# Stores begun by ScalarE's queue instead of SyncE's in a conformer, state-space and FFN block

## The chip, the cores and the metric

The kernel runs on one core of one Trainium2 chip. The metric is the device time of one execution in microseconds (us); the median of several runs is compared. Lower is better.

## The reference

One block of a streaming encoder works on 1024 tokens of width 1024, in float32. Its first half normalises the input, projects it, and runs two branches side by side: a gated convolution over 31 tokens with a layer norm, and a Mamba-2 scan (SSD) with 32 heads in 4 groups. Gates merge them. Its second half is a SwiGLU FFN. Both halves are modulated by the vector c (adaLN). Cut to what matters:

```python
shift, scale, gate = adaln(c, w_ada_mix, b_ada_mix)
h = rms_norm(x, norm_mix_w) * (1.0 + scale) + shift
conv_in, z, xbc, dt_raw, g_conv, g_ssm = split(h @ w_in)
u = a_half * sigmoid(b_half)                       # halves of conv_in
u = silu(layer_norm(causal_depthwise_conv(u, conv_dw_w, conv_dw_b)))
y_conv = u @ w_conv_out
xs, bm, cm = split(silu(causal_depthwise_conv(xbc, ssm_conv_w, ssm_conv_b)))
y = ssd_chunked_scan(xs, softplus(dt_raw + dt_bias), -exp(a_log), bm, cm) + d_skip * xs
y = group_rms_norm(y * silu(z)) * ssm_norm_w
y_ssm = y @ w_ssm_out
x = x + gate * ((sigmoid(g_conv) * y_conv + sigmoid(g_ssm) * y_ssm) @ w_out)
...
x = x + gate * ((silu(h @ w_gate) * (h @ w_up)) @ w_ffn_down)
return rms_norm(x, final_norm_w)
```

## The kernel before, in words

Channels lie on the 128 partitions and tokens in the free dimension. The tokens come in two halves of 512 (`hf` 0 and 1), so nearly every tile is 128x512. Each float32 product is made of three matmuls of rounded parts (`mm3`, L175 to L189): weight high by data high (L187), weight high by data low (L188), weight low by data high (L189). So each weight chunk of 128x1024 is loaded by a DMA (`load_w_`, L152), copied to its rounded form `wh` by ScalarE (L163) and subtracted to its rest `wl` by VectorE (L164), and then feeds 24 matmuls of TensorE for one output tile. The raw chunk has 2 buffers, the pairs wh and wl together 4 tiles, so two chunks can be ahead of TensorE.

The work comes in three parts. **Phase A** (about 100 to 600 us) makes most of the input projection for both halves at once by a seven-product scheme (`run_units`, matmuls at L817), with operands prepared by ScalarE (L795), GpSimd and VectorE (L796). Its results are finished by `z_done` (SiLU, L1160, stored to `z_d` at L1161), `g_done` and `gate0` (Tanh, L1166 and L1191, stored to `gt_d` at L1167 and L1192) and `SsmIn.conv` (a four-token convolution and a SiLU, L1133, stored to `xbc_d` at L1134). **Phase B** (about 600 to 1400 us) makes the rest of the projection with `mm3`, and beside it, in small steps between the weight matmuls, the SSD (`ssd`, L495 to L638), the convolution's layer norm (`conv_var`, `conv_norm`), the adaLN weights (`ada`, L245) and the norms. The SSD loads its inputs from `xbc_d` (L500), the decays M and E as broadcasts from `acs_d` (L550) and `eac_d` (L603), and the gate y from `z_d` (L605); its matmuls are bT (L510), cb (L517), xT (L570), st (L536), yo (L608) and yd (L623). ScalarE makes the exponentials of M (L557, L559) and the scaled inputs wx (L581). **The FFN** (from about 1400 us) uses the seven-product scheme again.

Intermediate results that don't fit are stored to DRAM and loaded again: `row_d` (a row of norm factors, stored at L297 in `bcast` and at once loaded as a broadcast at L299), `eac_d` (L486), `uc_d` (the convolution before centring, L702, and after, L723 in `conv_var`), `sp_d` (half a sum, L1291 in `smul`), `mp_d` (L1281) and `x1_d` (the residual, L1311 in `wout`). `conv_var` takes the mean off on VectorE (L721), squares on ScalarE (inside `add`, L320 or L325), stores the centred tile and loads the next. `wout` makes the residual in place on VectorE (`xr`, L1310), stores it, and squares it on ScalarE for the next norm.

All DMAs, loads and stores, are issued by SyncE's queue through one name, `dma = nc.sync.dma_start` (L104). Each engine and each queue works through its own list in order: an instruction that waits holds all behind it. The order of these lists is planned when the program is built, from the order of the code, from priorities (weight loads and splits are given one, L147 to L155) and from estimated times. So a change of one queue can move instructions of all engines. DMAs take one of eight counters (named DMAHW0 to DMAHW7) in turn, over all queues together, and each waits until the DMA that used its counter last has landed.

Of the kernel before, what the change touches and what calls it, by code (L numbers as in the profile page):

```python
# [70 lines left out]
def build(tc, ins, outs):  # L71
# [30 lines left out]
    mp = popen("a", "a")  # L102

    dma = nc.sync.dma_start  # L104
    act = nc.scalar.activation
    vec = nc.vector
    gp = nc.gpsimd
# [180 lines left out]
    def bcast(colsr, name, far=True):  # L288

        if far:  # L290
            pt = narrow("b" + name)
            nc.tensor.transpose(out=pt[0:NCK, 0:P], in_=colsr, identity=ident)
            q = stp.tile([P, P], F32, tag="brow", name="br" + name, bufs=1)
            act(out=q[0:NCK, :], in_=pt[0:NCK, 0:P], func=AF.Copy)
            i = nrow[0]
            nrow[0] += 1
            dma(out=row_d[i], in_=q[0:NCK, :])  # L297
            t = stp.tile([P, T], F32, tag="st", name="bc" + name)
            dma(out=t, in_=row_d[i:i + 1].rearrange("o c p -> o (c p)").to_broadcast([P, T]))  # L299
            return t  # L300
        pr = pstile("b" + name)
        for c in range(NCK):
            last = nc.tensor.matmul(out=pr[:, c * P:(c + 1) * P], lhsT=colsr[:, c:c + 1].to_broadcast([P, P]),
                                    rhs=ident, start=True, stop=True, skip_group_check=True)
        bcast.last, bcast.row = last.ins, pr
        t = stp.tile([P, T], F32, tag="st", name="bc" + name)
        act(out=t, in_=pr, func=AF.Copy)
        return t
# [100 lines left out]
    def dt_part(hf, wide, operands):  # L409

        D = DT[hf]

        n2 = KD * 32
        wd = wide("wd")[:, 0:n2]
        dma(out=wd, in_=wdt.rearrange("p k h -> p (k h)"))
        yield
        whl = wide("wdhl", F32R)
        wd_hi, wd_lo = whl[:, 0:n2], whl[:, n2:2 * n2]
        act(out=wd_hi, in_=wd, func=AF.Copy)
        vec.tensor_tensor(out=wd_lo, in0=wd, in1=wd_hi.bitcast(F32), op=ALU.subtract)  # L420
        yield
        yield
        pd = pstile(f"dt{hf}")
        n = len(operands)
        for j, (k, (rh, rl)) in enumerate(operands):
            wk = slice(k * 32, (k + 1) * 32)
            for i, (w, h) in enumerate(((wd_hi, rh), (wd_hi, rl), (wd_lo, rh))):
                nc.tensor.matmul(out=pd[0:32, :], lhsT=w[:, wk], rhs=h, start=j == 0 and i == 0,
                                 stop=j == n - 1 and i == 2)

        def sm(n):
            return pools["c"].tile([P, P], F32, name=f"dt_{n}{hf}")

        vt = wide("dtT")
        act(out=vt[0:32, :], in_=pd[0:32, :], func=AF.Copy)
        yield
        w4 = wide("dtw")
        v, s, q, u = (w4[:, i * P:(i + 1) * P] for i in range(4))
        dt = sm("dt")
        da = q  # L440
        pv = pstile(f"dtv{hf}")
        for c in range(NCK):
            nc.tensor.transpose(out=pv[:, c * 32:(c + 1) * 32], in_=vt[0:32, c * P:(c + 1) * P],
                                identity=ident[0:32, 0:32])
        vec.tensor_tensor(out=v.rearrange("p (c h) -> p c h", h=32),
                          in0=pv[:, :P].rearrange("p (c h) -> p c h", h=32),
                          in1=rw[:, 0:32].unsqueeze(1).to_broadcast([P, NCK, 32]), op=ALU.add)

        act(out=u, in_=v, func=AF.Abs)
        act(out=u, in_=u, func=AF.Exp, scale=-1.0)  # L450
        vec.tensor_scalar(out=s, in0=u, scalar1=2.0, scalar2=None, op0=ALU.add)
        vec.reciprocal(out=s, in_=s)
        vec.tensor_tensor(out=s, in0=s, in1=u, op=ALU.mult)
        vec.tensor_tensor(out=q, in0=s, in1=s, op=ALU.mult)
        vec.tensor_scalar(out=u, in0=q, scalar1=2.0 / 15, scalar2=2.0 / 13, op0=ALU.mult, op1=ALU.add)
        for d in (11, 9, 7, 5, 3, 1):
            vec.tensor_tensor(out=u, in0=u, in1=q, op=ALU.mult)
            vec.tensor_scalar(out=u, in0=u, scalar1=2.0 / d, scalar2=None, op0=ALU.add)
        vec.tensor_tensor(out=u, in0=u, in1=s, op=ALU.mult)
        vec.scalar_tensor_tensor(out=dt, in0=v, scalar=0.0, in1=u, op0=ALU.max, op1=ALU.add)  # L460
        vec.tensor_tensor(out=da.rearrange("p (c h) -> p c h", h=32),
                          in0=dt.rearrange("p (c h) -> p c h", h=32),
                          in1=nega.unsqueeze(1).to_broadcast([P, NCK, 32]), op=ALU.mult)
        for _ in range(12):
            yield
        pa = pstile(f"acs{hf}")
        nc.tensor.matmul(out=pa[:, 0:P], lhsT=tri, rhs=da, start=True, stop=True, skip_group_check=True)
        nc.tensor.matmul(out=pa[:, P:2 * P], lhsT=ones, rhs=da, start=True, stop=True, skip_group_check=True)
        acs, wdec, etot = (sm(n) for n in ("acs", "wdec", "etot"))
        vec.tensor_copy(out=acs, in_=pa[:, 0:P])  # L470
        act(out=etot, in_=pa[:, P:2 * P], func=AF.Exp)
        vec.tensor_tensor(out=wdec, in0=pa[:, P:2 * P], in1=acs, op=ALU.subtract)
        act(out=wdec, in_=wdec, func=AF.Exp)

        vec.tensor_tensor(out=wdec, in0=wdec, in1=dt, op=ALU.mult)
        yield
        pt = pstile(f"acsT{hf}")
        for c in range(NCK):
            nc.tensor.matmul(out=pt[0:32, c * P:(c + 1) * P], lhsT=da[:, c * 32:(c + 1) * 32], rhs=tri,
                             start=True, stop=True, skip_group_check=True)  # L480
        at = wide("acsT")
        vec.tensor_copy(out=at[0:32, :], in_=pt[0:32, :])
        dma(out=acs_d[hf], in_=at[0:32, :])
        et = wide("eacT")
        act(out=et[0:32, :], in_=pt[0:32, :], func=AF.Exp)
        dma(out=eac_d[hf], in_=et[0:32, :])  # L486
        D.update(dt=dt, acs=acs, wdec=wdec, etot=etot)


# [224 lines left out]
    def conv_var(hf):  # L714
        mean = bcast(mean_c[hf], f"mean{hf}")
        load = lambda i: xin(uc_d[hf, i], f"ud{hf}_{i}")
        t = load(0)
        yield 3
        q = SumSq(f"v{hf}", acc=spare.pop() if hf else None)
        for i in range(KD):  # L720
            vec.tensor_tensor(out=t, in0=t, in1=mean, op=ALU.subtract)  # L721
            q.add(t)
            dma(out=uc_d[hf, i], in_=t)  # L723
            t = load(i + 1) if i + 1 < KD else None
            yield 3
        yield 3
        q.rstd(1.0 / 1024, LN_EPS, out=r_ln[hf])
        yield 3
# [382 lines left out]
    class SsmIn(Sums):  # L1111
# [9 lines left out]
        def conv(self, src, m, hf, before=None):  # L1121
# [9 lines left out]
                    vec.scalar_tensor_tensor(out=t[:, :d], in0=before[:, T - d:], scalar=wc(k), in1=t[:, :d],  # L1131
                                             op0=ALU.mult, op1=ALU.add)
            act(out=t, in_=t, func=AF.Silu, scale=2.0)  # L1133
            dma(out=xbc_d[hf, i], in_=t)  # L1134

        def c11(self, s1, Y):
            add(s1, s1, Y)
# [19 lines left out]
    def phase_a():  # L1157
        def z_done(i):
            def f(t, src, m, hf):
                act(out=t, in_=src, func=AF.Silu)  # L1160
                dma(out=z_d[hf, i + m], in_=t)  # L1161
            return f

        def g_done(q, i):
            def f(t, src, m, hf):
                act(out=t, in_=src, func=AF.Tanh, scale=0.5)  # L1166
                dma(out=gt_d[hf, q, i + m], in_=t)  # L1167
            return f

        ci = [(CH_CI + 2 * i, CH_CI + 2 * i + 1, ConvIn(i)) for i in range(KD)]  # L1170
# [15 lines left out]
        def gate0(m):  # L1186
            def f(w):
                pt = xtile(m, f"p0_0{m}") if m < 4 else pstile(f"p0_0{m}")
                mm3(pt, w, W8, H)
                t = mp.tile([P, T], F32, tag="x0", name=f"ga{m}", bufs=2)  # L1190
                act(out=t, in_=pt, func=AF.Tanh, scale=0.5)  # L1191
                dma(out=gt_d[0, 0, m], in_=t)  # L1192
            step(f, CH_GC + m)

        def begin(_):
# [16 lines left out]
    def phase_b():  # L1212
# [32 lines left out]
        def gates1():  # L1245

            for m in range(N_GATE):
                def f(w, m=m):
# [1 line left out]
                    mm3(pt, w, W8, O)  # L1250
                    t = pools["b"].tile([P, T], F32, tag="xo", name=f"ga1_{m}", bufs=2)
                    act(out=t, in_=pt, func=AF.Tanh, scale=0.5)
                    dma(out=gt_d[1, 0, m], in_=t)
                step(f, CH_GC + m)

        def next_h(k, dst, rcol, name, src, gcol, mod, keep=False):
# [27 lines left out]
        def smul(hf, kc, m, ops, dst):  # L1284
            def f(w):
                pt = mmtile(f"s{hf}_{kc}{m}")
                mm3(pt, w, W8, ops)
                if kc == 0:
                    t = pools["b"].tile([P, T], F32, tag="xf", name=f"sp{hf}_{m}", bufs=N_XF)
                    act(out=t, in_=pt, func=AF.Copy)  # L1290
                    dma(out=sp_d[hf, m], in_=t)  # L1291
                    return
                a, gs, t = (L[f"{n}{hf}_{m}"] for n in ("spl", "gsl", "mpl"))
                vec.tensor_tensor(out=a, in0=a, in1=pt, op=ALU.add)
# [6 lines left out]
        def wout(hf, m, ops):  # L1301
            def f(w):
# [5 lines left out]
                pt = mmtile(f"wo{hf}_{m}")  # L1308
                mm3(pt, w, W8, ops)
                vec.scalar_tensor_tensor(out=xt, in0=pt, scalar=gate_h[:, m:m + 1], in1=xt, op0=ALU.mult, op1=ALU.add)  # L1310
                dma(out=x1_d[hf, m], in_=xt)  # L1311
                D[hf]["x1s"].add(xt)
                if m == KD - 1:
                    D[hf]["x1s"].rstd(1.0 / 1024, EPS, out=r_x1[hf])
            step(f, CH_WO + m, pre=[ahead(f"xr{hf}_{m}", xT[hf, :, m, :])])
# [458 lines left out]
```

## Time and profile before

| | us |
|---|---|
| median of 3 runs | 2086.82 |
| lowest and highest | 2083.7 and 2092.11 |
| the profiled execution | 2084.13 |
| its span in the trace | 2082.4 |
| granted TensorE clock, mean | 0.975 of full speed |
| DMA: read and written over the span | 281.57 and 83.13 MB |

The profile is one execution, in microseconds from the span's start. PE is TensorE's matmul, PEld its weight load, DVE VectorE, ACT ScalarE, POOL GpSimd, SP SyncE; SPq and ACTq are the queues of DMA issues. A line `L1291` is a line of the kernel before. A row of waits reads: who waited, at which line, for which engine's work on which tile; then the total, the number of times and the longest. A name like `out<-in` is the tile written and the tile read. The chain is followed back from the last instruction to what released each step.

### The profile page before, as it was taken

The page shows a single profiled execution, that of the slowest core. Times are in us where ns is not written, and L with a number is a line of the kernel's source. Part 1 is how long each engine was busy: PE and PEld are TensorE (multiplying, and loading weights), DVE is VectorE, ACT ScalarE, POOL GpSimd, SP SyncE. Part 2 cuts the span into 40 slices and gives each one's busy share as a digit, 9 for nine tenths or more (in the row PEclk, how much of TensorE's full clock was granted, in tenths as well). Part 3 has the DMA queues.
Part 4 walks back from the last instruction along what each step waited for, and adds up shares of the span by engine and source line. Part 5 has one row for each costly group of instructions (what it writes and reads, how often), then busy time and mean ns, then how long its engine had stood idle before and what let it go on. Part 6 is the DMA issues. An engine that isn't in the chain of part 4 may idle for free.

```text
span 2082.4 us, 26179 instructions
## 1 busy us (share of the span) xinstructions
PE 1941.3 (93%) x8802; PEld 1548.7 (74%) x8802; DVE 1574.0 (76%) x2458; ACT 1004.0 (48%) x1938; POOL 646.8 (31%) x487
## 2 busy tenths in 40 slices
PE   4899899999998899998899999998999999989997
PEld 3788688887876677776677777776888888767876
DVE  8878989878797978989797965759543443699655
ACT  4644454443444867566555733335333333444243
POOL 0008688888870000100000000005443443331400
PEclk9999999999998999999999999999999999999998
DMA  9232222323326867789898777761422222577653
GB/s 348 86 105 93 76 97 102 116 86 107 104 86 215 271 198 237 243 294 304 266 315 264 239 247 245 250 241 64 154 81 86 85 73 101 186 244 234 202 174 119
DMA packets 163958, 366.43 MB, mean 176 GB/s; under 512 B 18744, under 2 KB 19184, under 8 KB 163824
## 3 DMA queue, kind: packets, MB, share of 16 engines
q1 hardware_dynamic: 163824, 364.77, 52.6%
q8 instruction: 69, 1.13, 0.2%
q14 instruction: 65, 0.53, 0.1%
HBM read 281.57 MB, written 83.13 MB: 175 GB/s over the span
## 4 chain that ended last, share of the span: by engine, by line
PE 59%; DVE 20%; DMA 12%; issue 4%; ACT 3%; POOL 1%; SPq 0%; DVEq 0%; ACTq 0%; POOLq 0%
PE uXp L817 10%; PE uXf L817 10%; PE uZp L817 5%; PE uZf L817 5%; PE uXd L817 3%; PE uYp L817 2%; PE uYf L817 2%; DMA M<-acs_d 2%; PE s L189 2%; PE s L187 2%; PE s L188 2%; DMA E<-eac_d 2%; DMA wa_f<-in 1%; DVE gc L1128 1%; DMA wa_m<-in 1%
## 5 line engine op out<-in xcount | busy, mean ns | idle before, releaser
L163 ACT ACTIVATE wh<-w 128x1024 fp32r<-128x1024 f32 (+1 forms) x110 | 113.4, 1032 | 108.6 <-PE s L188 37.4
L164 DVE TENSOR_TENSOR wl<-w,wh 128x1024 fp32r<-128x1024 f32 (+1 forms) x110 | 130.7, 1189 | 23.3 <-ACT wh L163 15.8
L531 POOL TENSOR_TENSOR S<-S,dt_etot 128x512 f32<-128x512 f32 x16 | 20.5, 1281 | 294.7 <-ACT S L538 138.5
L557 ACT ACTIVATE M<-M,dt_acs 128x128 f32<-128x128 f32 x256 | 80.0, 394 | 59.4 <-DMA M<-acs_d 58.6
L930 POOL TENSOR_TENSOR fw<-fw,fw 128x512 f32<-128x512 f32 x37 | 59.5, 1608 | 120.2 <-DMA fw<-in 118.6
L672 DVE SCALAR_TENSOR_TENSOR pcM<-u,cw_eo,pcM 128x512 f32<-128x512 f32 x120 | 90.2, 752 | 2.5
L672 DVE SCALAR_TENSOR_TENSOR pcQ<-u,pc,pcQ 128x512 f32<-128x512 f32 x112 | 84.3, 753 | 2.7
L187 PE MATMUL s<-Hh,wh 128*128 128x512 f32 x192 | 76.4, 402 | 6.3 <-ACT Hh L217 4.0
L672 DVE SCALAR_TENSOR_TENSOR pcR<-u,pc,pcR 128x512 f32<-128x512 f32 x104 | 78.4, 754 | 2.7
L189 PE MATMUL s<-Hh,wl 128*128 128x512 f32 x192 | 76.8, 400 | 3.6 <-DVE wl L164 3.6
L187 PE MATMUL p<-Hh,wh 128*128 128x512 f32 x144 | 62.3, 453 | 18.0 <-DVE xo L1109 9.0
L188 PE MATMUL s<-Hl,wh 128*128 128x512 f32 x192 | 77.1, 402 | 0.9 <-DVE Hl L218 0.8
L845 POOL TENSOR_TENSOR b<-Hh,Hl 128x512 f32<-128x512 f32 x4 | 5.9, 1480 | 223.3 <-DVE spare L329 211.9
L817 PE MATMUL uXp<-T2h,dp 128*128 128x512 f32 x216 | 72.0, 395 | 3.0 <-ACT dp L795 3.0
L817 PE MATMUL uZp<-B22h,ep 128*128 128x512 f32 x216 | 72.4, 397 | 2.2 <-POOL ep L796 1.6
L817 PE MATMUL uYp<-Hh,bp 128*128 128x512 f32 x216 | 72.8, 399 | 1.0 <-DVE s1g L997 1.0
L817 PE MATMUL uXp<-T3h,fp 128*128 128x512 f32 x216 | 72.0, 396 | 1.2 <-ACT s L985 0.9
L817 PE MATMUL uXp<-T4h,gp 128*128 128x512 f32 x216 | 72.5, 396 | 0.4 <-DVE s5c L997 0.4
L817 PE MATMUL uZp<-T1h,cp 128*128 128x512 f32 x216 | 72.0, 395 | 0.0
L817 PE MATMUL uXp<-Hh,ap 128*128 128x512 f32 x216 | 71.0, 390 | 0.0
L188 PE MATMUL p<-Hl,wh 128*128 128x512 f32 x144 | 61.3, 427 | 5.4 <-DVE Hl L346 5.4
L817 PE MATMUL uZf<-T1h,cf 128*128 128x512 f32 x176 | 59.4, 401 | 3.5 <-DVE g L997 3.5
(565 smaller groups left out, 6412.5 us busy)
## 6 DMA issues: line engine op xcount, KB each, us to landing
fw<-in SPq DMA_DIRECT2D x134, 512.0 KB, 3.3
w<-in SPq DMA_DIRECT2D x100, 512.0 KB, 5.1
M<-acs_d SPq DMA_DIRECT2D x64, 256.0 KB, 4.9
wa_f<-in SPq DMA_DIRECT2D x48, 256.0 KB, 3.7
wa_m<-in SPq DMA_DIRECT2D x16, 512.0 KB, 9.3
xs<-xbc_d SPq DMA_DIRECT2D x32, 256.0 KB, 6.0
E<-eac_d SPq DMA_DIRECT2D x64, 128.0 KB, 6.2
y<-z_d SPq DMA_DIRECT2D x32, 256.0 KB, 5.5
```

Source lines behind the costliest of these rows:

```text
L163: act(out=hi, in_=w[:, :nk * P], func=AF.Copy)
L164: eng.tensor_tensor(out=lo, in0=w[:, :nk * P], in1=hi.bitcast(F32), op=ALU.subtract)
L187: nc.tensor.matmul(out=out, lhsT=whi[:, sl], rhs=rh, start=first and i == 0, stop=False)
L188: nc.tensor.matmul(out=out, lhsT=whi[:, sl], rhs=rl, start=False, stop=False)
L189: nc.tensor.matmul(out=out, lhsT=wlo[:, sl], rhs=rh, start=False, stop=last and i == n - 1)
L531: gp.tensor_tensor(out=v3(sn), in0=v3(S[c]), in1=heads(etot, c, g), op=ALU.mult)
L557: act(out=m[:, sl], in_=m[:, sl], func=AF.Relu, scale=-1.0, bias=acs[:, c * 32 + hd:c * 32 + hd + 1])
L672: vec.scalar_tensor_tensor(out=pt if k < n - 1 else out or pt, in0=src(k), scalar=w(k), in1=pt, op0=ALU.mult, op1=ALU.add)
L817: nc.tensor.matmul(out=out, lhsT=l[:, sl], rhs=r, start=first and k == 0 and i == 0, stop=k == 3 and i == 2, skip_group_check=True)
L845: gp.tensor_tensor(out=t, in0=H[k][0].bitcast(F32), in1=H[k][1].bitcast(F32), op=ALU.add)
L930: e[8].tensor_tensor(out=a21, in0=a11, in1=a21, op=ALU.subtract)
L1128: vec.scalar_tensor_tensor(out=t[:, d:], in0=src[:, :T - d], scalar=wc(k), in1=t[:, d:], op0=ALU.mult, op1=ALU.add)
```

## The change

A second name, `adma`, issues DMAs on ScalarE's own queue. 152 stores use it instead of `dma`: `row_d` (14), `eac_d` (2), the centred `uc_d` (16), `xbc_d` from `SsmIn.conv` (24), `z_d` (32), `gt_d` (20 in `g_done`, 6 in `gate0`, 6 in `gates1`), `sp_d` (16) and `x1_d` in `wout` (16). All loads stay on SyncE's queue, and so do the stores of `acs_d`, the uncentred `uc_d`, `y_d`, `mp_d`, `xbc_d` from `group`, and all stores of the FFN. In `wout` the store also changes places with the Square. One line is added near the top, so each later line's number is one higher in the changed kernel, and the store of `x1_d` goes from L1311 to L1313.

```diff
     dma = nc.sync.dma_start
+    adma = nc.scalar.dma_start
...
             act(out=q[0:NCK, :], in_=pt[0:NCK, 0:P], func=AF.Copy)
...
-            dma(out=row_d[i], in_=q[0:NCK, :])
+            adma(out=row_d[i], in_=q[0:NCK, :])
             t = stp.tile([P, T], F32, tag="st", name="bc" + name)
...
             vec.tensor_tensor(out=t, in0=t, in1=mean, op=ALU.subtract)
             q.add(t)
-            dma(out=uc_d[hf, i], in_=t)
+            adma(out=uc_d[hf, i], in_=t)
...
             act(out=t, in_=t, func=AF.Silu, scale=2.0)
-            dma(out=xbc_d[hf, i], in_=t)
+            adma(out=xbc_d[hf, i], in_=t)
...
                 act(out=t, in_=src, func=AF.Silu)
-                dma(out=z_d[hf, i + m], in_=t)
+                adma(out=z_d[hf, i + m], in_=t)
...
                     act(out=t, in_=pt, func=AF.Copy)
-                    dma(out=sp_d[hf, m], in_=t)
+                    adma(out=sp_d[hf, m], in_=t)
...
                 vec.scalar_tensor_tensor(out=xt, in0=pt, scalar=gate_h[:, m:m + 1], in1=xt, op0=ALU.mult, op1=ALU.add)
-                dma(out=x1_d[hf, m], in_=xt)
                 D[hf]["x1s"].add(xt)
+                adma(out=x1_d[hf, m], in_=xt)
```

ScalarE's list, before, where the residual of the first half begins. `wh` are weight copies, `xr` the residual tiles, M the SSD's decays, `un` and `say` tiles of the norms; in brackets stand the counters and engines that an instruction waits for:

```order
L163 ACTIVATE wh_9833<-w_9745 128x1024 [waits DMAHW0_49,PE_49]
L320 ACTIVATE spare_6227<-xr_0_9741 128x512 [waits DVE_49]
L557 ACTIVATE M_10014<-M_10014,dt_acs_6622 128x128 [waits DMAHW6_49]
L557 ACTIVATE M_10014<-M_10014,dt_acs_6622 128x128 x3
L163 ACTIVATE wh_9908<-w_9831 128x1024 [waits DMAHW3_49,PE_49]
L559 ACTIVATE M_10014<-M_10014 128x512 [waits Activation_49]
L557 ACTIVATE M_10016<-M_10016,dt_acs_6622 128x128 [waits DMAHW1_49]
L557 ACTIVATE M_10016<-M_10016,dt_acs_6622 128x128 x3
L559 ACTIVATE M_10016<-M_10016 128x512 [waits Activation_49]
L739 ACTIVATE un_0_9761<-un_0_9761,pc 128x512 [waits DVE_49]
L739 ACTIVATE un_1_9817<-un_1_9817,pc 128x512 [waits DVE_49]
L320 ACTIVATE say_9550<-y_9554 128x512 [waits DVE_49]
```

The same place after the change:

```order
L321 ACTIVATE spare_6227<-xr_0_9741 128x512 [waits DVE_49]
L1313 DMA x_d<-xr_0_9741 128x512 [waits DMAHW6_49]
L560 ACTIVATE M_9772<-M_9772 128x512 [waits Activation_49]
L560 ACTIVATE M_9774<-M_9774 128x512 [waits Activation_49]
L1313 DMA x_d<-xr_1_9743 128x512 [waits DMAHW6_49,DVE_49]
L164 ACTIVATE wh_9990<-w_9906 128x1024 [waits DMAHW5_49,PE_49]
L740 ACTIVATE un_0_9761<-un_0_9761,pc 128x512 [waits DVE_49]
L740 ACTIVATE un_1_9817<-un_1_9817,pc 128x512 [waits DVE_49]
L1313 DMA x_d<-xr_2_9829 128x512 [waits DMAHW5_49,DVE_49]
L164 ACTIVATE wh_10113<-w_9988 128x1024 [waits DMAHW1_49,PE_49]
```

The stores of the residual stand between the weight copies, each ahead of one; they wait for VectorE (DVE) and for a counter.

SyncE's list at that place, before:

```order
L1272 DMA xr_5_10109<-in 128x512 [waits DMAHW4_49,Activation_49]
L152 DMA w_9906<-in 128x1024 [waits DVE_49]
L605 DMA y_9642<-z_d 128x512 [waits DMAHW5_49]
L605 DMA y_9726<-z_d 128x512 [waits DMAHW6_49]
L605 DMA y_9846<-z_d 128x512 [waits DMAHW7_49]
L1311 DMA x_d<-xr_1_9743 128x512 [waits DMAHW0_49,DVE_49]
L603 DMA E_10251<-eac_d 64x512 [waits DMAHW1_49]
L152 DMA w_9988<-in 128x1024 [waits DMAHW2_49,DVE_49]
```

And after:

```order
L1273 DMA xr_5_10109<-in 128x512 [waits DMAHW7_49,DMAHW6_49,Activation_49]
L606 DMA y_9554<-z_d 128x512 [waits DMAHW0_49]
L153 DMA w_9988<-in 128x1024 [waits DMAHW1_49,DVE_49]
L606 DMA y_9642<-z_d 128x512 [waits DMAHW2_49]
L606 DMA y_9726<-z_d 128x512 [waits DMAHW3_49]
L606 DMA y_9846<-z_d 128x512 [waits DMAHW4_49]
L153 DMA w_10111<-in 128x1024 [waits DMAHW6_49,DVE_49]
L551 DMA M_10014<-acs_d 128x512 [waits DMAHW7_49,PE_49]
```

No store stands between the loads there any more, and the weight load w_9988 has moved ahead of three loads of y.

TensorE's list early in phase B, where the SSD's matmuls yd and yo stand among those of the weight chunks p_20 and p_21, before:

```order
L189 MATMUL p_20_5692<-Hh_117,wl_5610 128x512
L608 MATMUL yo_5458<-bc_20_5156,S_5250 128x128
L608 MATMUL yo_5458<-bc_20_5156,S_5321 128x128
L536 MATMUL st_5462<-wx_5384,btok_5177 128x512
L623 MATMUL yd_5476<-M_5240,xdt_5229 64x128
```

And after the change (its lines are one higher):

```order
L188 MATMUL p_21_5789<-Hh_111,wh_5688 128x512
L189 MATMUL p_21_5789<-Hl_112,wh_5688 128x512
L624 MATMUL yd_5476<-M_5240,xdt_5229 64x128
L609 MATMUL yo_5458<-bc_20_5156,S_5366 128x128
L624 MATMUL yd_5476<-M_5242,xdt_5229 64x128
```

The first 14 of p_21's 24 matmuls now come ahead of the eight yd of that tile. TensorE's list is the same in phase A, up to the start of phase B, and in the FFN.

More of the change, by code (lines that the diff above doesn't have):

```diff
@@ L485, in dt_part @@
         act(out=et[0:32, :], in_=pt[0:32, :], func=AF.Exp)
-        dma(out=eac_d[hf], in_=et[0:32, :])
+        adma(out=eac_d[hf], in_=et[0:32, :])
         D.update(dt=dt, acs=acs, wdec=wdec, etot=etot)
@@ L1166, in f @@
                 act(out=t, in_=src, func=AF.Tanh, scale=0.5)
-                dma(out=gt_d[hf, q, i + m], in_=t)
+                adma(out=gt_d[hf, q, i + m], in_=t)
             return f
@@ L1191, in f @@
                 act(out=t, in_=pt, func=AF.Tanh, scale=0.5)
-                dma(out=gt_d[0, 0, m], in_=t)
+                adma(out=gt_d[0, 0, m], in_=t)
             step(f, CH_GC + m)
@@ L1252, in f @@
                     act(out=t, in_=pt, func=AF.Tanh, scale=0.5)
-                    dma(out=gt_d[1, 0, m], in_=t)
+                    adma(out=gt_d[1, 0, m], in_=t)
                 step(f, CH_GC + m)
```

## The prediction

> **What bounds the kernel now.** I read the page's busy shares and its chain first, then the same times by stage, and only then the waits of the stages in which the moved stores lie. The page:
>
> ```profile
> PE 1941.3 (93%) x8802; PEld 1548.7 (74%) x8802; DVE 1574.0 (76%) x2458; ACT 1004.0 (48%) x1938; POOL 646.8 (31%) x487
> ...
> PE 59%; DVE 20%; DMA 12%; issue 4%; ACT 3%; POOL 1%; SPq 0%; DVEq 0%; ACTq 0%; POOLq 0%
> ```
>
> TensorE (PE) works 1941.3 of 2082.4 us, so all that any change of queues can win is 141 us. SyncE's queue itself (SPq) is 0% of the chain, ScalarE (ACT) 3%, transfers 12%. Next, busy time by stage. The columns are the stretch, then PE, PE's weight load, VectorE (DVE), ACT and GpSimd (POOL), the granted clock, the DMA share and GB/s:
>
> ```profile
> 0.00:100.00 100.00, 66.75 (x268) 52.42 (x268) 84.35 (x168) 56.74 (x96) 1.84 (x12) 0.97 0.61 224
> 100.00:600.00 500.00, 491.78 (x2114) 395.17 (x2115) 430.41 (x589) 223.04 (x376) 363.75 (x283) 0.99 0.29 98
> 600.00:1400.00 800.00, 733.43 (x3613) 574.93 (x3612) 640.69 (x1126) 450.57 (x1012) 55.18 (x52) 0.96 0.76 249
> 1400.00:2083.00 683.00, 649.29 (x2811) 526.21 (x2809) 418.58 (x577) 273.65 (x457) 225.99 (x141) 0.98 0.42 140
> ```
>
> PE idles 33 us at the start, 8.2 in phase A (100 to 600 us), 66.6 in phase B (600 to 1400) and 33.7 in the FFN (683.00 − 649.29). None of the moved stores lies in the FFN, about 75 lie before 600 us and about 77 after. So the question is phase B's 66.6 us. The waits of SyncE's queue (SP) there, as total us, times, longest:
>
> ```profile
> SPq L152 <- DVE wl L164: 64.9, 53, 4.6
> SPq L1311 <- DVE xr L1310: 20.5, 12, 4.0
> ...
> SPq L1134 <- ACT gc L1133: 15.2, 6, 4.1
> ...
> SPq L299 <- DMA row_d<-bry: 11.2, 7, 2.8
> ...
> SPq L723 <- DVE ud L721: 6.2, 9, 2.0
> ...
> SPq L1291 <- ACT sp L1290: 6.0, 5, 2.3
> ...
> SPq L297 <- ACT bry L294: 5.3, 3, 2.2
> ...
> SPq L297 <- ACT brmean L294: 4.1, 1, 4.1
> ```
>
> Moved stores held SP for 20.5 + 15.2 + 6.2 + 6.0 + 5.3 + 4.1 = 57.3 us by these rows, 7% of the stage. The longest row, the weight loads waiting for their buffer, stays, and so does the reload of a row that has just been stored (L299). And these are PE's own waits in phase B:
>
> ```profile
> PE p L187 <- DVE xo L1109: 10.7, 4, 8.5
> PE wo L187 <- ACT wh L163: 6.9, 3, 4.5
> PE yo L608 <- DVE E L613: 6.2, 2, 4.8
> ...
> PE s L187 <- ACT Hh L217: 4.0, 2, 3.5
> ...
> PE p L187 <- ACT wh L163: 3.2, 3, 1.4
> PE yd L623 <- DVE M L562: 3.1, 2, 1.6
> PE yd L623 <- ACT M L557: 2.9, 1, 2.9
> PE scy L264 <- DVE say L329: 2.4, 1, 2.4
> ...
> PE yo L608 <- DVE S L540: 2.2, 2, 1.7
> PE st L536 <- ACT wx L581: 1.9, 1, 1.9
> ...
> PE cb L517 <- DMA bc<-xbc_d: 1.0, 1, 1.0
> ```
>
> PE waits for VectorE and ScalarE; the one quoted wait that a transfer ends is 1.0 us. A late load reaches PE only through an engine between.
>
> **The change, part by part.** *SP loses 152 stores.* In phase A its holds were long:
>
> ```profile
> SPq L1134 <- ACT gc L1133: 85.1, 16, 13.0
> ...
> SPq L1167 <- ACT s1g L1166: 43.6, 5, 19.8
> ```
>
> Both rows are moved stores, 128.7 us for which SP no longer stands still. But PE is busy 491.78 of these 500 us, so at most 8.2 us can come of it. PE's longest wait there is for ScalarE, not for a load:
>
> ```profile
> PE uXp L817 <- ACT dp L795: 3.0, 1, 3.0
> ```
>
> I count the gain of phase A as 0; the matmuls already queued hide it. In phase B I take SP's freed share of PE's idle time: 57.3 / 800 of 66.6 = 4.8 us gained. The bounds are 0 (no load was on PE's path, as its waits suggest) and 18.7, all that the rows of the SSD (yo, yd, scy and st) add up to, since its loads are those that stood in line with the stores. I stay near the low end because PE's rows name engines.
>
> *ScalarE gains 152 stores.* What one takes is read from the 16 sp_d stores on SP, and from ScalarE at the place where they are made (start, duration, form, idle before):
>
> ```profile
> L1291 SPq DMA_DIRECT2D sp_d<-sp x16: 319/352/553, 976.2 to 1296.7; - x16
> ...
> DMA to landing us min/median/max: 3.8/4.3/4.8
> ```
> ```profile
> 1267.40 1.06 ACT L163 ACTIVATE wh<-w 128x1024 fp32r<-128x1024 f32 x1 [4.05 <-PE s L188]
> 1268.36 0.58 ACT L1290 ACTIVATE sp<-s 128x512 f32<-128x512 f32 x1
> 1273.00 1.06 ACT L163 ACTIVATE wh<-w 128x1024 fp32r<-128x1024 f32 x1 [4.05 <-DVE wl L164]
> ```
> ```profile
> 1268.97 0.33 SPq L1291 DMA_DIRECT2D sp_d<-sp  x1
> ```
>
> The issue takes 0.35 us (median of 16). The store waits for its activation's end at 1268.94 and starts 0.03 later. The next activation can then no longer start before this one has ended, as sp did 0.10 before wh's end (1268.46). Together 0.48 us for each store, if issuing costs ScalarE what it cost SP, which no row of before shows. 152 stores make 73 us, against 1078 us that ScalarE idles; 77 of them, 37 us, lie in phase B against 349 idle. Here, for example, ScalarE sat 4.05 us before each copy of weights, so this stage hides them. On PE's path ScalarE stood ten times in the rows above (wo 3, s 2, p 3, yd 1, st 1; 18.9 us). If a store stands ahead of every second one, the loss is 5 × 0.48 = 2.4 us; the bounds are 0 and all 37. In phase A ScalarE is 45% busy; 75 × 0.48 = 36 us there lies in its idle 277 us, and I count 0, with 3.6 as the end if every tenth store stood ahead of an operand that PE awaits.
>
> *The counters.* Each transfer still waits until the one eight places earlier on its counter has landed, now over both queues together. A store on ScalarE may thus wait for a load of SP, and ScalarE would wait with it. Before, the same wait stood on SP. I price it in the second rival, and at 0 in the sum, since the loads on the counters are mostly eight issues old.
>
> *The residual's store.* On SP it waited for VectorE (20.5 us in 12 waits). Now it stands on ScalarE, behind the Square of the same tile for m = 0, but, by the order, ahead of the next weight copy and of the later Squares for m = 1 to 3. Behind it wait the weight copies wh, after them wl on VectorE, and then PE. The same holds for the centred convolution's store, though it waits for less (6.2 us).
>
> *The order of PE.* The plan places the SSD's small matmuls differently among the weight matmuls: 14 rows of the weight block p_21 now stand before the eight yd matmuls. PE works the same number of us. Since these yd, yo, st and scy waits are in the rows above, the new places may remove or add them; in the sum they are 0, and the range has them on both sides.
>
> Sum: 2084.13 − 4.8 + 2.4 = 2081.7 us for an execution like the profiled one. That one lies 2.7 below the median of the runs shown, 2086.82, and since a median will be measured I put the 2.7 back: 2084 us. No change that can be told: a measurement of this kernel tells about 0.5% from none, 10.4 us here, so from 2076.4 to 2097.2.
>
> A rule that speaks against the change is in the Trainium skill (DMA: Bandwidth & Descriptors, Issuing engines are not separate DMA queues): all queues share the same transfer engines, and starting from several saves only the sequencer's starting time, usually small beside the transfer. By it the gain is 77 × 0.35 = 27 us of SP's time, 3% of the stage, so 2.2 us in place of 4.8, and the sum 2.6 higher. The trace agrees on the sizes, 0.35 against 4.3 us to landing, but its 57.3 us of waits in order are not in the rule.
>
> **The rivals.** *First, faster: freed loads and later SSD matmuls close the SSD's waits.* yo 6.2 + 2.2, yd 3.1 + 2.9, scy 2.4 and st 1.9 are those 18.7 us, in which PE stands for a result of the SSD chain, whose inputs (M, E, xs) are loads that stood behind moved stores on SP. If the loads come earlier by the stores' holds of 2 to 4 us and the small matmuls come later by 14 of the 24 matmuls of a weight chunk (of 5.6 us, from the two copies at 1267.40 and 1273.00, so 3.3 us), these waits go. That gives 2086.8 − 18.7 − 4.8 + 2.4 = 2066 us. For it: each single wait, at most 4.8 us, is about as long as a hold. Against it: what ends them is VectorE or ScalarE, busy 80% and 56%, and SP still waits 64.9 us in the weight loads. The Trainium skill (Perfetto Trace Analysis, DMA Optimizations) advises one queue for inputs and another for outputs; the trace bears this out only as far as SP's 57.3 us. Chance 0.37.
>
> *Second, slower: ScalarE is held by a store, and the next weight copy comes late.* What such a hold does stands in the trace already, where ScalarE waited for the load of M ahead of a weight copy in the stage of the residual:
>
> ```profile
> 1132.53 1.28 ACT L557 ACTIVATE M<-M,dt_acs 128x128 f32<-128x128 f32 x4 [2.80 <-DMA M<-acs_d]
> 1133.71 1.04 ACT L163 ACTIVATE wh<-w 128x1024 fp32r<-128x1024 f32 x1
> ```
> ```profile
> 1134.80 0.73 PE L187 MATMUL wo<-Oh,wh 128*128 128x512 f32 x1 [4.50 <-ACT wh L163]
> ```
> ```profile
> 1136.18 0.75 DVE L1310 SCALAR_TENSOR_TENSOR xr<-wo,gate_h,xr 128x512 f32<-128x512 f32 x1
> ```
> ```profile
> L164 DVE TENSOR_TENSOR wl<-w,wh 128x1024 fp32r<-128x1024 f32 (+1 forms) x110 | 130.7, 1189 | 23.3 <-ACT wh L163 15.8
> ```
>
> A hold of 2.80 and 1.28 us of other work cost PE 4.50. In the 5.6 us of a chunk the residual on VectorE takes 0.75, its store 0.35, wh 1.06 and wl 1.19, together 3.35, so 2.2 us are left: the rival decides once the store waits longer than that for VectorE or for a counter. 12 of the old waits on VectorE's xr averaged 1.7 us, the longest 4.0. Four such holds over the 16 residual and 16 convolution stores cost 4 × 4.5 = 18 us: 2084 + 18 = 2102 us. Against it: SP's wait was partly its own lateness, and the activation in front often waits as long. Chance 0.25.
>
> *Third: the change does nothing for loads,* because SP goes on standing at L152, L299 and the counters. Then only the 2.4 us remain: 2089 us, inside "no change", which with the sum has a chance of 0.38.
>
> **How the numbers follow.** No change that can be told is the likeliest, 0.38, and its number is 2084 us; its own range is 2077 to 2097. Faster (0.37) centres on 2066, slower (0.25) on 2102. Leaving out a tenth on either side cuts a quarter of the faster case, so the range begins at 2059, 7 below that case's centre (SP's share at 12 us in place of 4.8), and two fifths of the slower one, so it ends at 2105, 3 above its centre of four holds. Every issue on PE's path, +37 us, lies outside.
>
> **What would show each step.** The moved lines gone from SP's waits, and those of weight loads, xs, M and E not longer. The stores on ScalarE's queue at 0.3 to 0.4 us each. PE's busy time unchanged at 1941; its idle time in phase A within 8 ± 4 us, in phase B 64. The first rival is right if phase B falls by 20 us and the rows yo, yd, scy and st go. The second is right if rows "PE wo, s, co for ACT wh" grow beyond 20 us together and ScalarE's queue shows waits for VectorE's xr or ud, or for transfers, ahead of them. The forecast is wrong if phase A or the FFN, which I hold at 0, moves by more than 5 us, or if a store issued by ScalarE takes several times 0.35 us.

## The result and the profile after

The changed kernel takes 2102.79 us (median of 5, 2100.87 to 2107.23), against 2086.82 for the kernel before (median of 5): 16 us slower, a ratio of 1.0076 with a 95% interval of 1.0050 to 1.0103. The profiled execution is the one of 2102.79 us. Its page, busy shares and chain:

```profile
PE 1952.8 (93%) x8802; PEld 1553.7 (74%) x8802; DVE 1578.6 (75%) x2458; ACT 1005.5 (48%) x1938; POOL 645.5 (31%) x487
...
PE 56%; DVE 21%; DMA 12%; ACT 4%; issue 4%; POOL 1%; SPq 1%; ACTq 0%; DVEq 0%; POOLq 0%
```

TensorE runs the same 8802 matmuls, but is busy for 11.5 us longer (1941.3 before); 7.2 of the 18.7 us by which the span grew are idle. SyncE's queue makes 1% of the chain (0% before), ScalarE's 0%. ScalarE's busy time is nearly unchanged (1004.0 before). These are single executions, and those of one kernel lie several us apart: the one of before had a granted clock of 0.975, where 86 other executions of that kernel have a median of 0.972 and the five of the changed kernel one of 0.969. By these medians about 6 us of the 11.5 (0.003 of 2100, an estimate) belong to the kernel, the rest to the executions that were profiled.

Where does it happen? The first and last start of a tile's matmuls mark the stages (their durations stand ahead, as lowest, median and highest in ns). First the changed kernel, then the one before; `co` is the convolution's output product and `wo` the residual's:

```profile
L188 PE MATMUL co<-Hh,wh x128: 387/389/797, 853.8 to 1259.8; 128*128 128x512 f32 x128
L188 PE MATMUL wo<-Oh,wh x128: 387/393/750, 1118.3 to 1402.2; 128*128 128x512 f32 x128
```
```profile
L187 PE MATMUL co<-Hh,wh x128: 387/389/795, 852.3 to 1244.4; 128*128 128x512 f32 x128
L187 PE MATMUL wo<-Oh,wh x128: 390/394/795, 1114.3 to 1384.0; 128*128 128x512 f32 x128
```

Up to the first `co`, phase A included, 1.5 us are lost, at the first `wo` 4.0, at the last `co` 15.4, at the last `wo` 18.2. So 13.9 of the 18.7 us fall between 853.8 and 1260 us, and 2.8 more up to 1402. From there to the end 0.5 us are lost. Busy times from the first `co` to the end of phase B and then to the last FFN products, after (first fence) and before:

```profile
853.80:1402.70 548.90, 511.25 (x2513) 398.76 (x2512) 424.87 (x741) 283.87 (x643) 23.98 (x19) 0.96 0.79 259
1402.70:2010.70 608.00, 586.56 (x2534) 475.41 (x2533) 382.19 (x514) 244.14 (x418) 222.11 (x139) 0.99 0.42 144
```
```profile
852.30:1384.40 532.10, 497.26 (x2492) 393.01 (x2490) 416.89 (x731) 280.48 (x625) 25.11 (x19) 0.97 0.82 266
1384.40:1992.90 608.50, 587.39 (x2535) 475.40 (x2534) 381.62 (x514) 244.06 (x418) 223.49 (x139) 0.99 0.43 144
```

Of the 16.8 us that this stretch grew, 14.0 are TensorE's busy time and 2.8 its idle time. 21 matmuls more have slipped into it, about 4 us at the stage's mean of 0.20; most of the rest goes with the granted clock. Taken in windows of 10 us from 850 to 1400 us, what the clock lacked of full speed adds up to 24.0 us, and to 15.3 before; where TensorE idles meanwhile this costs nothing, so the 8.7 us between them are a bound. What pulls the clock down is seen at TensorE's longest pause there (start, duration, form, idle before):

```profile
969.19 0.39 PE L190 MATMUL s<-Hh,wl 128*128 128x512 f32 x1
975.03 0.79 PE L188 MATMUL s<-Hh,wh 128*128 128x512 f32 x1 [5.45 <-ACT sp L1291]
975.62 0.63 PE L189 MATMUL s<-Hl,wh 128*128 128x512 f32 x1
...
978.60 0.63 PE L190 MATMUL s<-Hh,wl 128*128 128x512 f32 x1
979.03 0.48 PE L188 MATMUL s<-Hh,wh 128*128 128x512 f32 x1
979.35 0.40 PE L189 MATMUL s<-Hl,wh 128*128 128x512 f32 x1
```

After 5.45 us of waiting nine matmuls take 4.0 us in place of the 2.1 that they take at the usual 0.23: the pause costs 5.45 and then 1.9 more. The Trainium skill (TensorE: Matmul & The Clock Gate, Part 1: The HAM clock gate) has the array's clock halve after an idle window of about 3.4 us and return after as long a busy one. This pause agrees. But the lowest clock of those 10 us windows needed no such pause:

```profile
1050.00:1060.00 10.00, 7.00 (x18) 3.96 (x19) 7.29 (x24) 7.85 (x30) 0.00 (x0) 0.54 0.79 229
```

The longest pauses between 1034 and 1067 us are 2.58, 1.40 and 1.19 us, so in this kernel shorter pauses brought the clock down too.

ScalarE at that moment shows who kept the copy `sp` waiting:

```profile
969.58 2.44 ACT L558 ACTIVATE M<-M,dt_acs 128x128 f32<-128x128 f32 x8 [3.51 <-PE s L190]
971.93 1.13 ACT L560 ACTIVATE M<-M 128x512 f32<-128x512 f32 x2
972.97 0.57 ACT L1109 ACTIVATE pre<-p 128x512 f32<-128x512 f32 x1
973.45 1.04 ACT L164 ACTIVATE wh<-w 128x1024 fp32r<-128x1024 f32 x1
974.39 0.58 ACT L1291 ACTIVATE sp<-s 128x512 f32<-128x512 f32 x1
975.00 0.33 ACTq L1292 DMA_DIRECT2D sp_d<-sp  x1
```

Not a store: the copy stands behind ten exponentials of M and a weight copy, by the order of the list. The store comes after it and takes 0.33 us. Of the stores of the residual, two held ScalarE for over a microsecond: one started 2.13 us after the activation ahead of it had ended, one 1.55 us. Here is the first:

```profile
1148.47 1.52 ACT L740 ACTIVATE un<-un,pc 128x512 f32<-128x512 f32 x2
1152.12 0.33 ACTq L1313 DMA_DIRECT2D x_d<-xr  x1
1156.45 1.06 ACT L164 ACTIVATE wh<-w 128x1024 fp32r<-128x1024 f32 x1 [6.45 <-DMA w<-in]
```

Even behind it the weight copy then waited 4.00 us more, for the weights' own load. Two centred convolution stores were held, for 1.61 and 1.70 us; all others of these two kinds, for 0.31 us or less. In the four windows of 10 us in which these holds lie (from 880, 900, 1150 and 1180 us) TensorE was busy for all 10 us.

SyncE's queue, finally, in phase B of the changed kernel (600 to 1410 us):

```profile
SPq L153 <- DVE wl L165: 94.7, 59, 4.5
SPq L153 <- POOL ep L797: 30.4, 2, 19.8
SPq L246 <- DVE as_f L250: 27.0, 18, 4.8
```

The 57.3 us of holds by moved stores are gone, and the weight loads now wait 94.7 us for their buffers (64.9 before): SyncE comes to the loads earlier and waits there.

### The profile page after: what moved, and what is told of

The parts are those of the page before. It is cut to its first block, busy times and chain, and to the rows that moved or that the text cites. A ratio compares the mean times of both kernels' runs of the same rounds, so it can differ in the third digit from the quotient of the medians.

```text
span 2101.1 us, 26072 instructions
## 1 busy us (share of the span) xinstructions
PE 1952.8 (93%) x8802; PEld 1553.7 (74%) x8802; DVE 1578.6 (75%) x2458; ACT 1005.5 (48%) x1938; POOL 645.5 (31%) x487
## 4 chain that ended last, share of the span: by engine, by line
PE 56%; DVE 21%; DMA 12%; ACT 4%; issue 4%; POOL 1%; SPq 1%; ACTq 0%; DVEq 0%; POOLq 0%
PE uXp L818 10%; PE uXf L818 10%; PE uZp L818 5%; PE uZf L818 5%; PE uXd L818 3%; PE uYp L818 2%; PE uYf L818 2%; DMA M<-acs_d 2%; PE s L189 2%; PE s L190 2%; PE s L188 2%; DVE gc L1129 2%; DVE wl L165 1%; PE uZd L818 1%; PE fd L190 1%
## 5 line engine op out<-in xcount | busy, mean ns | idle before, releaser
L164 ACT ACTIVATE wh<-w 128x1024 fp32r<-128x1024 f32 (+1 forms) x110 | 113.7, 1034 | 136.7 <-PE s L189 57.3
L188 PE MATMUL p<-Oh,wh 128*128 128x512 f32 x144 | 58.6, 407 | 8.9 <-DVE xo L1110 8.9
```

The source lines that it names most:

```text
L164: act(out=hi, in_=w[:, :nk * P], func=AF.Copy)
L188: nc.tensor.matmul(out=out, lhsT=whi[:, sl], rhs=rh, start=first and i == 0, stop=False)
```

## The experiments

Theory A: the cost lies in the new order of the lists, which the planner made when the stores left SyncE's queue. Theory B: it lies in the stores themselves, on ScalarE's queue. In several runs lists are held to an order that was recorded from a kernel: after all instructions are known, each instruction of an engine is tied to come after its predecessor in the record. This orders their issue; it adds no work.

```diff
+def pin(tc):
+    traced = {i.name: i for i in tc.nc.cur_bb.bb.instructions}
+    for engine, names in ORDER.items():          # recorded lists
+        for a, b in zip(names, names[1:]):
+            tc.add_manual_dep(traced[b], a, NoSync, reason="pin")
...
         pclose(k)
+    pin(tc)
     es.close()
```

All ratios are to the kernel before, run on the same chip beside them. "Moved" counts TensorE's matmuls, of the 8254 in the program's list (the profile has 8802 records of them), that stand at another place than before, and the largest shift.

| run | stores on ScalarE's queue | moved | median us (before) | ratio, 95% interval |
|---|---|---|---|---|
| the change | 152 | 1899, 102 | 2102.79 (2086.82) | 1.0076, 1.0050 to 1.0103 |
| queue_new_order_old | 152 | 0 | 2092.02 (2088.67) | 1.0021, 1.0008 to 1.0033 |
| queue_old_order_new | 0 | 1899, 102 | 2102.86 (2088.67) | 1.0072, 1.0053 to 1.0092 |
| phase_a_stores | 84 | 1816, 102 | 2086.78 (2088.67) | 0.9993, 0.9977 to 1.0008 |
| phase_b_stores | 68 | 1684, 86 | 2095.49 (2088.67) | 1.0035, 1.0021 to 1.0049 |
| six_gate_stores | 6 | 1438, 151 | 2106.20 (2089.26) | 1.0081, 1.0058 to 1.0105 |
| stores_that_keep_order | 56 | 0 | 2092.01 (2089.26) | 1.0025, 1.0009 to 1.0042 |
| sp_copy_first | 152 | 1899, 102 | 2103.87 (2089.26) | 1.0071, 1.0044 to 1.0097 |
| weight_copy_first | 0 | 0 | 2090.88 (2089.26) | 1.0003, 0.9987 to 1.0019 |
| pace_0_90_before | 0 | 974, 403 | 2105.53 (2087.31) | 1.0087, 1.0070 to 1.0104 |
| pace_0_86_before | 0 | 925, 292 | 2089.66 (2087.31) | 1.0012, 0.9998 to 1.0026 |
| pace_0_90_after | 152 | not compared | 2100.14 (2087.31) | 1.0067, 1.0050 to 1.0085 |
| tensor_order_old | 152 | 0 | 2097.23 (2087.31) | 1.0052, 1.0035 to 1.0070 |
| scalar_vector_order_old | 152 | 266, 18 | 2096.71 (2087.19) | 1.0039, 1.0022 to 1.0055 |
| load_order_old | 152 | 1165, 51 | 2116.88 (2087.19) | 1.0140, 1.0116 to 1.0164 |

**Queue and order apart.** Both kernels with all five lists held to the other's order (`ORDER` holds the lists of all engines and SyncE's list without the moved stores, which the planner places).

> All 152 stores are on ScalarE's queue as after the change, but TensorE, VectorE, ScalarE, GpSimd and SyncE's loads are held to the order of the kernel before. If the 16 us came from the new order of the lists (theory A), this runs within 5 us of before, about 2084 to 2090 us, and TensorE's mean granted clock is back from 0.969 to about 0.975. If they came from stores on ScalarE's queue, their issue time and holds (theory B), it stays near 2103 us. A result between the two divides the loss.

> All stores are on SyncE's queue as before, but the engines and SyncE's loads are held to the order that the changed kernel has. Theory A: about 2103 us, slower than before by 16 us, with the same pauses of TensorE at the places of the changed kernel. Theory B: about 2087 us. If both this and the run with the old order are slow, queue and order each cost something.

The new order alone costs 0.72% and the new queue alone, in the old order, 0.21%; with the new order the queue adds nothing that shows (1.0076 and 1.0072). So about 14 us of the 16 are the order. TensorE's waits in phase B with the new order and the old queue carry the changed kernel's signs, a wait for `sp` and one for the convolution's `Hh`:

```profile
PE co L187 <- ACT Hh L747: 5.5, 1, 5.5
...
PE s L187 <- ACT sp L1290: 4.2, 1, 4.2
```

With the old order and the new queue (from 852 us on) the waits of before are back, 6.9 for the weight copy of `wo` and 4.8 for E there:

```profile
PE wo L188 <- ACT wh L164: 7.3, 4, 4.6
...
PE yo L609 <- DVE E L614: 5.1, 2, 5.0
```

The clock was expected back at 0.975 with the old order; the profiled execution had 0.973, and the one with the new order 0.973 too, so the mean clock of a single execution does not tell the two apart. Over all executions it averages 0.971 with the new order (6) and 0.972 with the old (12).

**Parts of the change.** The order is planned anew in each.

```diff
 # phase_a_stores: row_d, uc_d, the second half's gt_d, sp_d and x1_d back on SyncE's queue
 # phase_b_stores: eac_d, xbc_d, z_d, phase A's gt_d back on SyncE's queue
-adma(out=...)
+dma(out=...)
```

> Only the stores of xbc_d, z_d, eac_d and gt_d of phase A (84 of 152) are moved; those of phase B stay on SyncE's queue, and the order is planned anew. Theory A: the time is that of whatever order phase B gets, anywhere from 2080 to 2110 us, and phase A itself keeps its length within 2 us. Theory B: 2087 to 2090 us, since these stores lie where ScalarE idles over half the time and TensorE is 98% busy.

> Only the stores of row_d, the centred uc_d, gt_d of the second half, sp_d and x1_d (68 of 152) are moved, with the order planned anew. Theory B: about 2103 us, as the stores that stand among the weight copies are those that hold ScalarE. Theory A: again the time of the order that phase B gets, 2080 to 2110 us, without relation to the number of stores.

These two do not decide it alone: 84 stores cost nothing that shows, though they move TensorE's list about as far as the whole change does, 68 cost 0.35%, and the parts do not add up to the whole. The next two say more.

```diff
 # six_gate_stores, from the kernel before
-dma(out=gt_d[1, 0, m], in_=t)
+nc.scalar.dma_start(out=gt_d[1, 0, m], in_=t)
 # stores_that_keep_order, from the kernel before: z_d, gt_d[0, 0, m], eac_d, sp_d
```

> The kernel before with only the six gt_d stores of the second half moved to ScalarE's queue, and the order planned anew. Six issues of 0.33 us are 2 us of ScalarE at the most (theory B: 2087 to 2091 us). But the plan moves 1438 of TensorE's 8254 matmuls by up to 151 places. Theory A: the time is that of another order, outside 2085 to 2092 us more likely than inside, on either side.

> The kernel before with 56 stores moved to ScalarE's queue: z_d (32), gt_d of the first six gates (6), eac_d (2) and sp_d (16). The order of TensorE's list comes out the same as before, place by place, without being held. Theory A: within 3 us of before, 2086 to 2092 us, 56 stores notwithstanding. Theory B: about a third of the 16 us, 2093 to 2095 us.

Six stores, issued at 763 to 813 us in the changed kernel, cost 0.81%, as much as all 152; 56 stores that leave TensorE's order as it was, and ScalarE's and the loads' too, cost 0.25%. In the run with the six, the wait that stands out between 850 and 1400 us (1.0 us before) is at yet another place:

```profile
PE cb L517 <- DMA bc<-xbc_d: 11.8, 3, 7.1
```

**A single pause.** One place of one list is changed, everything else is held.

```diff
 # sp_copy_first, in the order of the changed kernel: ScalarE's list
+sp_0 (L1291)
 M exponentials of two tiles (L558, L560), pre (L1109), wh (L164)
-sp_0 (L1291)
 # weight_copy_first, in the order of before: ScalarE's list
+wh_9908 (L163)
 four M exponentials (L557)
-wh_9908 (L163)
```

> The changed kernel with all lists held as they are, but for one place: in ScalarE's list the copy of the first sp tile goes ahead of the exponentials of two M tiles (ten instructions) that wait for their load there. TensorE waited 5.45 us at that place for this copy, and its clock was at 0.66 of full speed for about 4 us behind it. If that order is what costs (theory A), the wait falls below 1 us, the clock stays up, and the kernel gains 4.5 + 2 = 6 to 7 us, about 2096 us. If the wait only moves on, because VectorE or the SSD is the limit behind it, it stays at 2101 to 2104 us.

> The kernel before with all lists held as they are, but for one place: in the stage of the first residual the weight copy goes ahead of four exponentials of M, which waited 2.80 us for their load, and behind which TensorE waited 4.50 us. All stores stay on SyncE's queue. Theory A: the wait goes, with the drop of the clock behind it, and the kernel gains 4 to 6 us, about 2083 us against 2088. If the weight's own load or the SSD is late anyway, it stays within 2 us of before.

Both pauses went as meant, and neither run shows the gain. In the first, TensorE now waits 0.69 us for `sp`:

```profile
973.33 0.50 PE L188 MATMUL s<-Hh,wh 128*128 128x512 f32 x1 [0.69 <-ACT sp L1291]
```

but the wait for the convolution's Hh at 1218 us has grown from 3.02 to 5.14:

```profile
1218.50 1.22 PE L188 MATMUL co<-Hh,wh 128*128 128x512 f32 x2 [5.14 <-ACT Hh L748]
```

That growth need not come from the edit: in queue_old_order_new, the same order with the pause for `sp` left in (4.2 us), this wait was 5.5 us. The median is that of the changed kernel, but the interval (from 1.0044) just reaches the 6 us that were expected, and the profiled execution, 2095.91, is the fastest of the six; so this run does not decide it. In the second the wait for the weight copy fell from 4.50 to 0.66 us, and one for E took its place:

```profile
1139.01 0.50 PE L187 MATMUL wo<-Oh,wh 128*128 128x512 f32 x1 [0.66 <-ACT wh L163]
...
1144.93 1.33 PE L623 MATMUL yd<-M,xdt 128*64 128x128 f32 x10 [3.72 <-DVE E L613]
```

There the interval ends at 0.9987, 2.7 us faster than before at the most, where 4 to 6 were expected. So taking away a visible pause need not shorten the kernel by it.

**Orders without any change of queue.**

```diff
-SSD_RATE = 0.85
+SSD_RATE = 0.90   # pace_0_90_before and pace_0_90_after; 0.86 in pace_0_86_before
```

> The kernel before with SSD_RATE 0.90 in place of 0.85 and all stores on SyncE's queue. Only the order changes, 974 of TensorE's matmuls by up to 403 places. Theory A: the time moves by more than 5 us to either side though no queue changes. If orders are worth little by themselves, 2085 to 2092 us.

> The kernel before with SSD_RATE 0.86 and all stores on SyncE's queue: 925 of TensorE's matmuls move by up to 292 places. As with 0.90: theory A lets the time move by 5 us or more to either side without any change of a queue; else it stays at 2085 to 2092 us. The two paces together show how far orders spread.

> The changed kernel with SSD_RATE, the pace at which SSD steps are mixed among the weight matmuls, 0.90 in place of 0.85; the queues are those of the change. In the changed kernel the stage of the first residual held 68 more matmuls of the SSD than before, so the SSD was behind. If that lag is the loss, a faster pace wins back 8 us or more, 2095 us or less. If any new order draws its own time, it lies anywhere from 2080 to 2115 us; if the stores cost (theory B), it stays at 2103.

With 0.90 the kernel before loses 0.87% with every store still on SyncE's queue, as much as the change costs, and TensorE waits most for the convolution:

```profile
PE co L187 <- ACT Hh L747: 16.5, 2, 13.0
```

With 0.86 it loses too little to tell. The faster pace did not rescue the changed kernel (2100.14). But set beside the kernel before at the same pace (2105.53, on the same chip) it is 5 us faster, and four of its five executions lie below all four of the other: at 0.90 the same change of queues comes out as a gain. So even the sign of the change hangs on the order that is planned around it. Whether the SSD's lag costs time stays open, since a faster pace is also another order.

**Which list.** All stores on ScalarE's queue, some lists held to the old order.

> All 152 stores on ScalarE's queue; only TensorE's list is held to the order of before, and the plan places the other engines' lists and SyncE's loads around it. If TensorE's own order carries the loss, it runs like the kernel with all lists held, 2089 to 2095 us. If the other engines' lists carry it, 2100 us or more.

> All 152 stores on ScalarE's queue; the lists of ScalarE, VectorE and GpSimd are held to the order of before, TensorE's and SyncE's lists are planned around them (266 of TensorE's matmuls then stand up to 18 places off the old order). If the lists of ScalarE and VectorE carry the loss, it runs like the kernel with all lists held, 2089 to 2095 us; if it needs TensorE's or SyncE's exact order too, 2097 us or more.

> All 152 stores on ScalarE's queue; only SyncE's list, the loads and the stores that stay, is held to the order of before, the engines' lists are planned around it. If the order of the loads carries the loss, 2089 to 2095 us; if the engines' lists do, 2100 us or more, as with TensorE's list alone held (2097).

No single list, held, brings the time back. TensorE's list held leaves 0.52%, ScalarE's, VectorE's and GpSimd's 0.39%, and SyncE's list alone, with the engines planned anew around it, is the slowest of all at 1.40%; only all together come down to 0.21%. Which list of the changed kernel costs the time these runs cannot say: the lists that are not held come out in a third order (with TensorE's list held, some 400 of ScalarE's 1928 activations still stand at another place than before).

No version here beats the kernel before; phase_a_stores equals it.

## Why the prediction was wrong

**Phase A, the FFN: right.** Both were put at 0; up to the first `co` 1.5 us were lost, from the end of phase B on 0.5. Neither of the two signs by which I said the forecast would be wrong appeared: these parts moved by less than 5 us, and a store took 0.33 us. Both signs left out the order.

**The gain on SyncE: wrong.** I took 4.8 us from 57.3 us of freed holds. In the old order no gain shows: moving 152 stores gave 1.0021, moving 56 gave 1.0025. The holds went and longer waits for weight buffers took their place (84.8 us in phase B with the old order and the new queue, 64.9 before), as the third rival said.

**The loss on ScalarE: it fits.** The issue takes 0.33 us and follows the activation by 0.03, as costed. Gain and loss together were put at −2.4; in the old order they measured +3.4 us (2092.02 against 2088.67; the interval is about 2 to 7 us), which fits the loss of 2.4 without the gain. The two were not measured apart. The profiled executions of these two kernels, 11.6 us apart, differ by 11.4 between the first `co` and the end of phase B; what costs it there was not tried.

**The order: the step that failed.** "the new places may remove or add them; in the sum they are 0": I put the rearranged lists at 0 because no row of before shows them, and priced them only where they would win, at 18.7 us in the first rival. It measured +14 us. Two things were missed. First, I weighed the new places of TensorE's list alone, but the change also moves 819 of ScalarE's 1928 activations and 875 of VectorE's 2458 instructions, and in the runs no single list, held to the old order, brought the time back. Second, I expected TensorE's busy time unchanged, "1941"; but the clock fell behind pauses, so that a pause costs busy time as well as idle time (+11.5 and +7.2 us in the profiled execution, a part of the 11.5 being that execution's).

**The first rival: its waits went, its time did not come.** The SSD's waits of 18.7 us fell to 7.9 in phase B (yo 1.2, yd 4.2, st 1.1, and 1.4 for `say`). The new places removed waits, as that rival had it, but others came in their place, the 5.4 us for `sp` among them, and TensorE's idle time grew by 7.2 us over all.

**The second rival: right in time by luck, wrong in mechanism.** It gave 2102 us for four holds of ScalarE by a store, and 2102.79 was measured. Two of the residual's stores and two of the convolution's did hold ScalarE for over a microsecond, but none over the 2.2 us from which I said it decides; TensorE did not stand still in the 10 us of any of them, and its waits for weight copies did not grow (the row of `wo` fell from 6.9 to 2.4 us). With no store on ScalarE's queue the new order alone gave 2102.86.

With the order held, no run here shows a gain from parting loads and stores. The Trainium skill (DMA: Bandwidth & Descriptors, Issuing engines are not separate DMA queues) says that starting transfers from several engines saves only the starting time, and these runs agree.

What stays open is what makes one order better than another: neither the longest pauses nor the pace of the SSD have been shown to explain it.

## What to carry to other kernels

Where a planner orders the lists, moving a few transfers to another queue is two changes: measure the queue with the lists held to the old order, and the new order with the old queue, before either is credited. Six stores were enough to move this kernel by 0.8%, and at another pace of the SSD the same change of queues came out as a gain, so a single gain or loss of that size says nothing of the queue. A pause that ends in one place may only move to the next, so judge an order by its time and not by its longest wait.

## What the runs showed of the hardware

A store started by ScalarE took 0.33 us of its queue (0.35 on SyncE), and the next activation mostly began 0.04 to 0.10 us behind it where it was ready. Behind 15 of the 152 stores the next activation began before the issue had ended, so the 0.48 us of the prediction are too much for those; here both start together:

```profile
1398.39 0.33 ACTq L1313 DMA_DIRECT2D x_d<-xr  x1
1398.39 0.61 ACT L326 ACTIVATE sqx<-xr 128x512 f32<-128x512 f32 x1
```

A pause of TensorE of 5.45 us was followed by 4.0 us at about half its matmul rate; pauses of 2.58 us and less came before 10 us with a mean clock of 0.54.
